# Transposed attention weights kept in their own tiles, and one stretch of value products per unit

## The chip, the cores and the metric

The kernel runs on one core of a Trainium2 chip. The metric is the device time of one execution in microseconds (us). Everything below is read from one profiled execution of the kernel before, and from its three timed runs.

## The reference, cut to what matters

A two-layer backbone over 1024 latent tokens and 256 context tokens, model width 1024, all in fp32. Each layer has two sub-layers. The first projects the tokens, runs three head groups beside each other (a gated mixer, a windowed attention, a differential attention) and projects their outputs back; the second is a gated MLP with a small convolution. Two of the head groups are attention, and only their last step is touched here:

```python
# B: windowed attention, 8 query heads over 2 kv heads, head width 64
p = softmax(concatenate([s_win, s_ctx, s_sink], axis=-1))
o = einsum('bnhgqk,bnkhd->bnqhgd', p_win, vb) + einsum('bnhgqk,bkhd->bnqhgd', p_ctx, v_ctx)
# C: differential attention, 4 heads, value width 64, all 1280 keys (context tokens read 256)
pd = p[:, :, 0] - lam * p[:, :, 1]
o  = einsum('bhqk,bkhd->bqhd', pd, v)
```

## The kernel before, in words

The kernel is written as a data-flow program; a scheduler orders the instructions of every engine when the kernel is built, by its own estimate of when each becomes ready, with the program's order as priority. So attention, which stands early in the program, is laced with matmuls of the projections and the MLP wherever attention isn't ready. On the chip each engine then follows its own fixed list.

Attention works in units over pairs of 128-token query tiles (`nq` is 2 everywhere). In `units_b` a unit is one kv head of one pair (18 units), and each unit has two blocks (`hp`), each with two query heads; a query tile sees 2 to 5 key tiles of 128. In `units_c` a unit is one head of one pair (36 units); a query tile sees 10 key tiles, or 2 for the context pair.

The path of a unit is the same in both. TensorE writes scores into PSUM tiles `S`; VectorE copies them negated into score tiles in SBUF with a running minimum (`negmax`, L496); ScalarE turns them into exponentials in place (L587, L703); in C, VectorE combines the two maps into the first one (L709). The score tiles are `pb` (B, one per query tile and block) and `ec` (C, two per query tile, `es[0]` and `es[1]`); both come from the same ring of four buffers, tag "e". They hold queries on partitions and keys in columns, and the value product needs keys on partitions. So `outputs` transposes them with TensorE, 128x128 at a time, into one of two PSUM tiles `T` (L609 in B, L734 in C); ScalarE copies a `T` tile into an SBUF tile `PT` (L613, L736), of which there are three; and TensorE multiplies the values with it into the PSUM tile `O` (L619, L725), accumulating over the key tiles. A product holds 64 value columns as weights, and the two query tiles of a pair go to partitions 0 to 63 and 64 to 127 of `O`. Transposes and products alternate: while ScalarE copies step k, TensorE is meant to do the products of step k-1. At the end of a B unit, four more matmuls with 64 weight columns (L629, `bc`) spread the reciprocal sums, and the result goes through `ob` and `stb`, which share the three buffers of tag "PT".

A `T` step in B is one key tile of both query tiles and both heads; in C it is four key tiles of one query tile. Matmuls of the projections and the MLP write PSUM tiles `z` and `zS` (L130, L132).

Of the kernel before, what the change touches and what calls it, by code (L numbers as in the profile page):

```python
# [10 lines left out]
F32 = mybir.dt.float32  # L11
F32R = mybir.dt.float32r
BF16 = mybir.dt.bfloat16
AF = mybir.ActivationFunctionType
# [18 lines left out]
P = 128  # L33
# [19 lines left out]
def trunk(ctx: ExitStack, tc: tile.TileContext, a: dict):  # L53
    nc = tc.nc
    act, dve, pool, pe, sp = nc.scalar, nc.vector, nc.gpsimd, nc.tensor, nc.sync

    def mkpool(name, bufs, side="left", space=None):
        kw = {"space": space} if space is not None else {}
        return tc.alloc_tile_pool(name=name, bufs=bufs, side=side, reuse_waits="tile", **kw)
# [10 lines left out]
    ident = cst[:, 0:P]  # L70
# [17 lines left out]
    st = {"wd": 0}  # L88
# [19 lines left out]
    def sub(eng, lo, src, hi):  # L108
        eng.tensor_tensor(out=lo, in0=src, in1=hi.bitcast(F32), op=ALU.subtract)  # L109
# [397 lines left out]
    def units_b(L, tiles, at, mkS, mkT, mkO):  # L507
# [3 lines left out]
        nq = len(tiles)  # L511
        cc = nwt * P
        info = []
# [5 lines left out]
        def unit(g):  # L519
# [24 lines left out]
            def scores():  # L544
# [3 lines left out]
                for hp in range(2):  # L548
                    pp = []
                    for ti, n in enumerate(tiles):  # L550
# [40 lines left out]
                        for j in (2 * hp, 2 * hp + 1):  # L591
                            pool.tensor_scalar(out=dgs[ti][:, j], in0=ident, scalar1=ls[:, j:j + 1], scalar2=None,  # L592
                                               op0=ALU.mult)
                    outputs(hp, pp)

            def outputs(hp, pp):
                V = both["V"]
                if hp == 0:
                    u["po"] = mkO()
                po = u["po"]  # L600
                prev = None
                for kk in range(max(len(x_[1]) for x_ in info) + 1):
                    tis = [ti for ti in range(nq) if kk < len(info[ti][1])]
                    new = None
                    if tis:
                        tp = mkT()
                        for m, ti in enumerate(tis):
                            for j in range(2):
                                pe.transpose(tp[:, (2 * m + j) * P:(2 * m + j) * P + P],  # L609
                                             pp[ti][:, j, kk * P:kk * P + P], ident)  # L610
                        PT = at.tile([P, 512], F32, tag="PT", name="PT", bufs=3)
                        w_ = 256 * len(tis)
                        act.activation(out=PT[:, :w_], in_=tp[:, :w_], func=AF.Copy)  # L613
                        new = (kk, tis, PT)
                    if prev is not None:
                        pk, ptis, pPT = prev
                        for m, ti in enumerate(ptis):
                            ix = info[ti][1]
                            pe.matmul(po[64 * ti:64 * ti + 64, 256 * hp:256 * hp + 256],  # L619
                                      V[:, ix[pk], 64 * g:64 * g + 64], pPT[:, 256 * m:256 * m + 256],  # L620
                                      start=(pk == 0), stop=(pk == len(ix) - 1))
                    prev = new
                if hp == 0:
                    return
                dgs = u["dg"]
                np_ = 64 * nq
                bc = mkT()
                for ti in range(nq):
                    pe.matmul(bc[64 * ti:64 * ti + 64, :], ones[:, 0:64], dgs[ti].rearrange("p j t -> p (j t)"),  # L629
                              start=True, stop=True)  # L630
                ob = at.tile([P, 512], F32, tag="PT", name="ob", bufs=3)
                act.activation(out=ob[:np_], in_=po[:np_], func=AF.Copy)
                dve.tensor_tensor(out=ob[:np_], in0=bc[:np_], in1=ob[:np_], op=ALU.mult)
                st = [at.tile([P, 512], F32R, tag="PT", name="stb", bufs=3) for _ in range(2)]
                act.activation(out=st[0][:np_], in_=ob[:np_], func=AF.Copy)
                sub(pool, st[1][:np_], ob[:np_], st[0][:np_])
                for ti, n in enumerate(tiles):
                    for h in range(2):
                        r0 = 256 + 256 * g
                        sp.dma_start(out=o_s[L][h, r0:r0 + 256, n * P:n * P + P].rearrange("(g d) t -> d g t", d=64),  # L640
                                     in_=st[h][64 * ti:64 * ti + 64].bitcast(F32).rearrange("d (g t) -> d g t", t=P))
# [6 lines left out]
    def units_c(L, hd, groups, at, mkS, mkT, mkO):  # L648
        kall = groups[0][0] < NLT
        k0 = 0 if kall else SEQ  # L650
        nk = NT - k0
        nkt = nk // P
        head = {}

        def unit(gi, tiles):
            nq = len(tiles)
# [22 lines left out]
            def scores():  # L679
# [3 lines left out]
                for ti in range(nq):  # L683
# [8 lines left out]
                    for bank in full[:h] + [rest] + full[h:]:  # L692
# [4 lines left out]
                        for b, (m, o, w_) in enumerate(bank):  # L697
# [4 lines left out]
                            if left[m] == h + 1:  # L702
# [7 lines left out]
                                                    in1=es[0][:, :nk], op0=ALU.mult, op1=ALU.add)  # L710
                    Ps.append(es[0])
                outputs(Ps)

            def outputs(Ps):
                V = head["V"]
                po = mkO()
                todo = [(q0, ti) for q0 in range(0, nkt, 4) for ti in range(nq)]
                PTs, ready = {}, []

                def pv():  # L720
                    q0 = ready.pop(0)
                    nb = min(4, nkt - q0)
                    for b in range(nb):
                        for ti in range(nq):
                            pe.matmul(po[64 * ti:64 * ti + 64, 0:P], V[:, q0 + b, :],  # L725
                                      PTs[q0, ti][:, b * P:b * P + P],
                                      start=(q0 + b == 0), stop=(q0 + b == nkt - 1))
                    return nb * 233.0

                for q0, ti in todo:  # L730
                    nb = min(4, nkt - q0)
                    tp = mkT()
                    for b in range(nb):
                        pe.transpose(tp[:, b * P:b * P + P], Ps[ti][:, (q0 + b) * P:(q0 + b) * P + P], ident)  # L734
                    PT = PTs[q0, ti] = at.tile([P, 512], F32, tag="PT", name="PT", bufs=3)
                    act.activation(out=PT[:, :nb * P], in_=tp[:, :nb * P], func=AF.Copy)  # L736
                    cost = nb * 107.0
                    if ready:
                        cost += pv()
                    if ti == nq - 1:  # L740
                        ready.append(q0)
                pv()
                nr = 64 * nq
                on = at.tile([P, P], F32, tag="on", name="on")
                act.activation(out=on[:nr], in_=po[:nr, 0:P], func=AF.Copy)
                tail(on)
# [168 lines left out]
    def finish(L, G, xg, mp):  # L915
# [5 lines left out]
        for (tok, xc, n) in G["out"]:  # L921
            for o in range(0, n, P):
# [24 lines left out]
               out=[(0, 0, 127), (SEQ, 128, 256)]),  # L947
# [4 lines left out]
               out=[(511, 0, 513)])]  # L952
# [14 lines left out]
    mkT = lambda: psT.tile([P, 512], F32, tag="T", name="T", bufs=2)  # L967
# [106 lines left out]
    at = mkpool("at0", 2, "left")  # L1074
# [105 lines left out]
    at = mkpool("at1", 2, "left")  # L1180
# [102 lines left out]
```

## Time and profile before

| | us |
|---|---|
| median of three timed runs | 3327.45 (3325.96 to 3328.93) |
| profiled execution, its own time | 3326.23 |
| span of the profiled execution | 3324.4 |
| TensorE matmul busy | 3146.2 (95%) |
| TensorE weight load busy | 2745.6 (83%) |
| VectorE busy | 2348.0 (71%) |
| ScalarE busy | 1744.8 (52%) |
| GpSimd busy | 888.1 (27%) |

The span is the time from the first to the last recorded instruction; the execution's own time has 1.83 us more. Matmuls are pipelined, so a matmul's duration in a row is longer than the step from one matmul to the next; where a cost on TensorE matters, it is read from starts, not from durations.

### The profile page before, as it was taken

How to read it: one execution, taken by the hardware profiler on the slowest of the kernel's cores; microseconds unless marked ns; L12 is line 12 of the kernel's file. 1: busy time of each engine (PE TensorE's matmuls, PEld its weight loads, DVE VectorE, ACT ScalarE, POOL GpSimd, SP SyncE). 2: the span in 40 equal slices, each digit the busy share in tenths (PEclk: the TensorE clock that was granted, in tenths of full speed). 3: DMA queues.
4: the chain of work that ended last, by engine and by line, in shares of the span. 5: the costliest groups of instructions: out<-in, count | busy, mean ns of one | idle time of the engine just before them, and what ended most of it. 6: DMA issues, size and time to landing. Idle time of an engine off the chain costs nothing. (4 is left out here: it accounts for less than half of the span.)

```text
span 3324.4 us, 54575 instructions
## 1 busy us (share of the span) xinstructions
PE 3146.2 (95%) x19503; PEld 2745.6 (83%) x19503; DVE 2348.0 (71%) x5306; ACT 1744.8 (52%) x3059; POOL 888.1 (27%) x1170
## 2 busy tenths in 40 slices
PE   7999989899999999999999899999999999999999
PEld 4776556787898889988999777767887789999999
DVE  5776666766878695878776678748776685666666
ACT  3554545655556563646444345557665564454443
POOL 1545211123222470127101054222322323222000
PEclk8999999899999999999999999999999999999999
DMA  8655786344533763378333556455645536434433
GB/s 270 187 162 156 225 250 180 86 128 122 136 106 89 241 177 114 105 199 238 102 96 113 169 144 171 125 150 151 163 138 152 135 110 195 122 106 137 137 114 109
DMA packets 754127, 499.52 MB, mean 150 GB/s; under 512 B 81480, under 2 KB 697792, under 8 KB 753856
## 3 DMA queue, kind: packets, MB, share of 16 engines
q1 hardware_dynamic: 753856, 496.03, 52.2%
q8 instruction: 155, 2.54, 0.3%
q14 instruction: 116, 0.95, 0.1%
HBM read 432.48 MB, written 63.44 MB: 149 GB/s over the span
## 5 line engine op out<-in xcount | busy, mean ns | idle before, releaser
L130 PE MATMUL z<-h,wsp 128*128 128x386 f32 (+3 forms) x5280 | 872.9, 319 | 17.2 <-ACT wsp L115 4.3
L130 PEld LDWEIGHTS z<-h,wsp 128*128 128x128 f32 x5280 | 823.8, 190 | 34.0 <-issue 11.4
L115 ACT ACTIVATE wsp<-raw 128x1024 fp32r<-128x1024 f32 (+2 forms) x660 | 556.0, 845 | 414.1 <-PE z L130 181.7
L109 DVE TENSOR_TENSOR wsp<-raw,wsp 128x1024 fp32r<-128x1024 f32 (+2 forms) x516 | 566.3, 1100 | 101.8 <-ACT wsp L115 98.5
L130 PE MATMUL z<-g,wsp 128*128 128x386 f32 (+3 forms) x2640 | 453.8, 320 | 18.0 <-DVE t L874 5.3
L130 PEld LDWEIGHTS z<-g,wsp 128*128 128x128 f32 x2640 | 412.9, 190 | 33.2 <-issue 10.0
L132 PE MATMUL z<-wsp,h 128*128 128x512 f32 x1584 | 401.1, 400 | 13.3 <-ACT zs L435 4.8
L109 POOL TENSOR_TENSOR wsp<-raw,wsp 128x128 fp32r<-128x128 f32 x528 | 253.7, 513 | 485.6 <-ACT wsp L115 439.4
L132 PEld LDWEIGHTS z<-wsp,h 128*128 128x128 f32 x1584 | 291.2, 190 | 80.3 <-ACT zs L435 7.0
L130 PE MATMUL zS<-h,wsp 128*128 128x386 f32 (+1 forms) x2112 | 334.2, 314 | 11.2 <-DVE t L874 4.3
L130 PEld LDWEIGHTS zS<-h,wsp 128*128 128x128 f32 x2112 | 319.0, 191 | 14.5 <-ACT wsp L115 5.1
L867 ACT ACTIVATE t<-z,cw 128x386 f32<-128x386 f32 (+3 forms) x220 | 137.8, 627 | 220.1 <-PE z L130 219.0
L871 DVE SCALAR_TENSOR_TENSOR t<-z,cw,t 128x255 f32<-128x255 f32 (+3 forms) x264 | 132.6, 502 | 150.9 <-ACT t L867 150.8
L496 DVE TENSOR_SCALAR_CACHE_REDUCE ec<-S,nmc 128x512 f32<-128x512 f32 (+1 forms) x256 | 173.9, 679 | 71.3 <-PE S L695 68.2
L171 POOL TENSOR_TENSOR mev<-mev,mtr 128x512 f32<-128x512 f32 x112 | 176.9, 1593 | 136.9 <-ACT mtr L170 134.1
L703 ACT ACTIVATE ec<-ec,nmc 128x1280 f32<-128x1280 f32 (+1 forms) x144 | 182.2, 1266 | 58.9 <-DVE ec L496 56.0
L130 PE MATMUL z<-oT,wsp 128*128 128x384 f32 (+2 forms) x1056 | 201.3, 337 | 2.5 <-DMA oT<-o_s 2.5
L899 DVE SCALAR_TENSOR_TENSOR xg<-z,mods,xg 128x384 f32<-128x384 f32 (+5 forms) x288 | 139.9, 501 | 81.3 <-PE z L130 79.9
L130 PE MATMUL zS<-g,wsp 128*128 128x386 f32 (+1 forms) x1056 | 181.8, 316 | 8.7 <-ACT g L884 4.0
L130 PEld LDWEIGHTS z<-oT,wsp 128*128 128x128 f32 x1056 | 178.8, 190 | 10.1 <-ACT zs L435 2.0
L381 POOL TENSOR_TENSOR rs<-ss,cst 128x8 f32<-128x8 f32 (+1 forms) x76 | 117.4, 1545 | 241.3 <-DVE ss L379 157.0
L592 POOL TENSOR_SCALAR dgb<-cst,ls 128x128 f32<-128x128 f32 x144 | 92.0, 652 | 317.9 <-DVE ls L590 168.1
(248 smaller groups left out, 4811.4 us busy)
## 6 DMA issues: line engine op xcount, KB each, us to landing
raw<-in_w_up_dram SPq DMA_DIRECT2D x264, 512.0 KB
mraw<-in_w_ada_dram SPq DMA_DIRECT2D x96, 512.0 KB
raw<-in_w_down_dram SPq DMA_DIRECT2D x192, 256.0 KB
Kc<-qk_s SPq DMA_DIRECT2D x96, 320.0 KB
raw<-in_w_in_dram SPq DMA_DIRECT2D x52, 512.0 KB
raw<-in_w_out_dram SPq DMA_DIRECT2D x48, 512.0 KB
raw<-in_w_down_dram SPq DMA_DIRECT2D x104, 192.0 KB
qk_s<-st SPq DMA_DIRECT2D x18, 512.0 KB
```

The costliest lines, as they stand in the source:

```text
L109: eng.tensor_tensor(out=lo, in0=src, in1=hi.bitcast(F32), op=ALU.subtract)
L115: act.activation(out=hl[:, 0], in_=raw, func=AF.Copy)
L130: pe.matmul(ps, w(i, k), h(j, k), start=s, stop=e)
L132: pe.matmul(ps, h(i, k), w(j, k), start=s, stop=e)
L171: pool.tensor_tensor(out=acc[s], in0=acc[s], in1=pr, op=ALU.add)
L381: pool.tensor_tensor(out=rs[:, :ns], in0=ss[:, 1, :ns], in1=mhalf[:, :ns], op=ALU.pow)
L496: dve.tensor_scalar(out=neg, in0=s_ap, scalar1=-1.0, scalar2=init, op0=ALU.mult, op1=ALU.min, accum_out=acc)
L592: pool.tensor_scalar(out=dgs[ti][:, j], in0=ident, scalar1=ls[:, j:j + 1], scalar2=None, op0=ALU.mult)
L703: act.activation(out=es[m][:, :nk], in_=es[m][:, :nk], func=AF.Exp, scale=-1.0, bias=acc[m], accum_out=l1[:, m, ti:ti + 1])
L867: act.activation(out=t[:, o:o + n], in_=ps[:, :n], func=AF.Identity, scale=cw[:, L, 1, ft:ft + 1], bias=cw[:, L, 3, ft:ft + 1])
L871: dve.scalar_tensor_tensor(out=t[:, o + b + 1:o + e], in0=ps[:, b:e - 1], scalar=cw[:, L, 0, ft:ft + 1], in1=t[:, o + b + 1:o + e], op0=AL ...
L899: dve.scalar_tensor_tensor(out=xs, in0=ps[:, b + o0:b + o1], scalar=mods[:, L, 40 + ct, s:s + 1], in1=xs, op0=ALU.mult, op1=ALU.add)
```

## The change

In both functions the copies that ScalarE makes of the transposed weights no longer go to a `PT` tile: they overwrite the score tile's own columns that were just transposed. All transposes and copies of a unit (in B: of a block) stand first, and after them all its products with the values, beginning with the last key tile and the last query tile, and with the pair's two query tiles side by side. In B a `T` tile now holds two key tiles of one query tile instead of one key tile of both. `ob` and `stb` get buffers of their own (one each, `stb` twice as wide), which take the 6 KB a partition that the three `PT` buffers had.

```diff
@@ units_b, outputs @@
-                prev = None
-                for kk in range(max(len(x_[1]) for x_ in info) + 1):
-                    tis = [ti for ti in range(nq) if kk < len(info[ti][1])]
-                    new = None
-                    if tis:
+                for k0 in range(0, max(len(x_[1]) for x_ in info), 2):
+                    for ti in range(nq):
+                        nb = min(2, len(info[ti][1]) - k0)
+                        if nb <= 0:
+                            continue
                         tp = mkT()
-                        for m, ti in enumerate(tis):
-                            for j in range(2):
-                                pe.transpose(tp[:, (2 * m + j) * P:(2 * m + j) * P + P],
-                                             pp[ti][:, j, kk * P:kk * P + P], ident)
-                        PT = at.tile([P, 512], F32, tag="PT", name="PT", bufs=3)
-                        w_ = 256 * len(tis)
-                        act.activation(out=PT[:, :w_], in_=tp[:, :w_], func=AF.Copy)
-                        new = (kk, tis, PT)
-                    if prev is not None:
-                        pk, ptis, pPT = prev
-                        for m, ti in enumerate(ptis):
-                            ix = info[ti][1]
+                        for j in range(2):
+                            for b in range(nb):
+                                pe.transpose(tp[:, (j * nb + b) * P:(j * nb + b + 1) * P],
+                                             pp[ti][:, j, (k0 + b) * P:(k0 + b + 1) * P], ident)
+                        act.activation(out=pp[ti][:, :, k0 * P:(k0 + nb) * P],
+                                       in_=tp[:, :2 * nb * P].rearrange("p (j c) -> p j c", j=2), func=AF.Copy)
+                for b in range(max(len(x_[1]) for x_ in info)):
+                    for ti in reversed(range(nq)):
+                        ix = info[ti][1]
+                        kk = len(ix) - 1 - b
+                        if kk >= 0:
                             pe.matmul(po[64 * ti:64 * ti + 64, 256 * hp:256 * hp + 256],
-                                      V[:, ix[pk], 64 * g:64 * g + 64], pPT[:, 256 * m:256 * m + 256],
-                                      start=(pk == 0), stop=(pk == len(ix) - 1))
-                    prev = new
+                                      V[:, ix[kk], 64 * g:64 * g + 64], pp[ti][:, :, kk * P:kk * P + P],
+                                      start=(b == 0), stop=(kk == 0))
...
-                ob = at.tile([P, 512], F32, tag="PT", name="ob", bufs=3)
+                ob = at.tile([P, 512], F32, tag="ob", name="ob", bufs=1)
...
-                st = [at.tile([P, 512], F32R, tag="PT", name="stb", bufs=3) for _ in range(2)]
+                st = at.tile([P, 2, 512], F32R, tag="stb", name="stb", bufs=1)
+                st = [st[:, 0], st[:, 1]]
@@ units_c, outputs @@
-                todo = [(q0, ti) for q0 in range(0, nkt, 4) for ti in range(nq)]
-                PTs, ready = {}, []
-                def pv():
...
-                for q0, ti in todo:
-                    nb = min(4, nkt - q0)
-                    tp = mkT()
-                    for b in range(nb):
-                        pe.transpose(tp[:, b * P:b * P + P], Ps[ti][:, (q0 + b) * P:(q0 + b) * P + P], ident)
-                    PT = PTs[q0, ti] = at.tile([P, 512], F32, tag="PT", name="PT", bufs=3)
-                    act.activation(out=PT[:, :nb * P], in_=tp[:, :nb * P], func=AF.Copy)
-                    cost = nb * 107.0
-                    if ready:
-                        cost += pv()
-                    if ti == nq - 1:
-                        ready.append(q0)
-                pv()
+                for q0 in range(0, nkt, 4):
+                    for ti in range(nq):
+                        nb = min(4, nkt - q0)
+                        tp = mkT()
+                        for b in range(nb):
+                            pe.transpose(tp[:, b * P:b * P + P], Ps[ti][:, (q0 + b) * P:(q0 + b) * P + P], ident)
+                        act.activation(out=Ps[ti][:, q0 * P:(q0 + nb) * P], in_=tp[:, :nb * P], func=AF.Copy)
+                for kt in reversed(range(nkt)):
+                    for ti in reversed(range(nq)):
+                        pe.matmul(po[64 * ti:64 * ti + 64, 0:P], V[:, kt, :], Ps[ti][:, kt * P:kt * P + P],
+                                  start=(kt == nkt - 1), stop=(kt == 0))
```

## Rows read from the trace of the kernel before

**Rows 1.** The page, part 1: busy time, share of the span, instructions.

```profile
PE 3146.2 (95%) x19503; PEld 2745.6 (83%) x19503; DVE 2348.0 (71%) x5306; ACT 1744.8 (52%) x3059; POOL 888.1 (27%) x1170
```

**Rows 2.** Windows of attention stages: PE, PEld, DVE, ACT, POOL busy; PEclk; DMA.

```profile
560.00:680.00 120.00, 102.38 (x598) 83.40 (x596) 91.91 (x250) 75.00 (x141) 22.10 (x28) 0.86 0.41 110
680.00:840.00 160.00, 159.43 (x990) 129.41 (x989) 101.98 (x299) 89.02 (x162) 44.46 (x84) 1.00 0.49 129
840.00:960.00 120.00, 118.90 (x737) 107.83 (x736) 94.22 (x231) 66.31 (x109) 19.40 (x35) 1.00 0.45 123
...
2140.00:2300.00 160.00, 149.10 (x1036) 105.72 (x1037) 97.61 (x341) 102.55 (x202) 42.93 (x57) 0.97 0.58 162
2300.00:2440.00 140.00, 130.44 (x1050) 117.09 (x1049) 118.25 (x287) 89.80 (x162) 38.27 (x75) 1.00 0.57 153
```

**Rows 3.** Tile O: the products, durations in ns (least/median/most), first and last start.

```profile
L725 PE MATMUL O<-PT,Vc x1312: 272/273/477, 195.6 to 2750.5; 128*64 128x128 f32 x188
...
L619 PE MATMUL O<-PT,Vb x640: 379/430/690, 288.4 to 2622.1; 128*64 128x256 f32 x160
```

**Rows 4.** Timeline of PE in a B block: start us, us, what, count.

```profile
341.56 0.66 PE L609 MATMUL T<-cst,pb 128*128 128x128 f32 x4
342.14 0.65 PE L619 MATMUL O<-PT,Vb 128*64 128x256 f32 x4
342.72 0.44 PE L609 MATMUL T<-cst,pb 128*128 128x128 f32 x2
```

**Rows 5.** Timeline of PE around a longer B stretch.

```profile
310.61 1.08 PE L619 MATMUL O<-PT,Vb 128*64 128x256 f32 x8
311.62 1.09 PE L609 MATMUL T<-cst,pb 128*128 128x128 f32 x8
```

**Rows 6.** Timeline of PE in a C unit.

```profile
881.01 1.09 PE L725 MATMUL O<-PT,Vc 128*64 128x128 f32 x14
882.03 0.87 PE L734 MATMUL T<-cst,ec 128*128 128x128 f32 x6
882.83 0.43 PE L725 MATMUL O<-PT,Vc 128*64 128x128 f32 x2
883.20 3.91 PE L130 MATMUL z<-h,wsp 128*128 128x384 f32 x21
...
892.64 0.65 PE L725 MATMUL O<-PT,Vc 128*64 128x128 f32 x6
893.22 1.48 PE L130 MATMUL z<-h,wsp 128*128 128x384 f32 x7
```

**Rows 7.** Timeline of PE: first and last of 192 C stretches.

```profile
195.56 0.43 PE L725 MATMUL O<-PT,Vc 128*64 128x128 f32 x2 [0.47 <-ACT PT L736]
...
2750.09 0.65 PE L725 MATMUL O<-PT,Vc 128*64 128x128 f32 x6
```

**Rows 8.** Timeline of PE: first and last of 171 B stretches.

```profile
288.36 0.65 PE L619 MATMUL O<-PT,Vb 128*64 128x256 f32 x4
...
2621.85 0.59 PE L619 MATMUL O<-PT,Vb 128*64 128x256 f32 x2
```

**Rows 9.** Groups by line and shape: the copies of T (busy us, mean ns; idle before).

```profile
L613 ACT ACTIVATE PT<-T 128x512 f32<-128x512 f32 x152 | 88.8, 592 | 95.7 <-PE T L609 82.4 <-DMA o_s<-stb 8.5 <-POOL stb L109 4.4
...
L736 ACT ACTIVATE PT<-T 128x512 f32<-128x512 f32 x128 | 73.9, 592 | 46.5 <-PE T L734 42.1 <-DMA o_s<-stb 1.8 <-DMA qc<-qk_s 1.8
...
L736 ACT ACTIVATE PT<-T 128x256 f32<-128x256 f32 x72 | 27.3, 380 | 46.2 <-PE T L734 46.1
```

**Rows 10.** Waits of VectorE: engine, line, for what: us in total, times, longest.

```profile
DVE pb L561 <- PE T L609: 42.6, 25, 9.0
...
DVE ec L496 <- PE T L734: 13.9, 13, 2.7
DVE pb L561 <- PE T L734: 13.8, 9, 4.3
```

More of the change, by code (lines that the diff above doesn't have):

```diff
@@ L716, in outputs @@
                 po = mkO()
-                todo = [(q0, ti) for q0 in range(0, nkt, 4) for ti in range(nq)]
-                PTs, ready = {}, []
-                def pv():
-                    q0 = ready.pop(0)
-                    nb = min(4, nkt - q0)
-                    for b in range(nb):
[L724 to L728, printed above, removed]
-                for q0, ti in todo:
-                    nb = min(4, nkt - q0)
-                    tp = mkT()
-                    for b in range(nb):
-                        pe.transpose(tp[:, b * P:b * P + P], Ps[ti][:, (q0 + b) * P:(q0 + b) * P + P], ident)
-                    PT = PTs[q0, ti] = at.tile([P, 512], F32, tag="PT", name="PT", bufs=3)
-                    act.activation(out=PT[:, :nb * P], in_=tp[:, :nb * P], func=AF.Copy)
-                    cost = nb * 107.0
-                    if ready:
-                        cost += pv()
-                    if ti == nq - 1:
-                        ready.append(q0)
-                pv()
+                for q0 in range(0, nkt, 4):
[9 more added lines that the diff above has]
+                                  start=(kt == nkt - 1), stop=(kt == 0))
                 nr = 64 * nq
```

## The prediction

> **What bounds the kernel now.** I read the page's busy times first. TensorE's matmuls cover 95% of the span, VectorE 71%, ScalarE 52% [rows 1]; the reader should note that this is an average over very different stages, and that a busy TensorE isn't yet a TensorE doing products. So next come the windows of the stages with attention [rows 2]. In 680 to 840 and 840 to 960 TensorE is busy for 159.43 of 160 and 118.90 of 120 us, at a granted clock of 1.00 (the 2.4 GHz level): whatever attention leaves free is filled with matmuls of the projections and the MLP. In 2140 to 2300 and 2300 to 2440 it idles for 10.9 of 160 and 9.6 of 140 us. In 560 to 680 it idles for 17.6 of 120 us, at a clock of 0.86. In the same windows VectorE is at 61 to 84% and ScalarE at 55 to 64%. So mostly TensorE is the limit, the others close enough behind that its idle time would grow if its work shrank.
>
> The third view is the order on TensorE, where one sees what the busy time is made of. Four transposes between two stretches of products take 0.58 us from start to start, six take 0.80 [rows 4, 6]: 0.11 each, and 0.14 once. Four B products take 0.58, eight take 1.01 [rows 4, 5]: two products for the two query tiles run together in 0.215, and 0.15 comes on top once. C products take 0.37, 0.58 and 1.02 for two, six and fourteen [rows 6]: 0.11 per two, and 0.26 once. The fixed parts belong to the change between matmuls with 128 and with 64 weight columns: each excursion to the products and back costs about 0.15 + 0.14 = 0.29 us in B and 0.26 + 0.14 = 0.40 in C, in which no result is made. That the fixed part of C is 0.11 larger, just one pair, suggests (an estimate) that in each C stretch two products of one query tile follow each other and don't run together.
>
> How often does that happen? Going through the whole timeline I counted 192 stretches of C products [rows 7] and 171 of B products [rows 8]. There are 1312 and 640 products [rows 3], so a stretch has 6.8 or 3.7 products on average, while a full C unit has 20 and a full B block up to 10.
>
> **The change, part by part.** *Alternation removed.* Now the excursions cost 192 x 0.40 = 77 us and 171 x 0.29 = 50 us, 127 us of TensorE time. After it the first product needs the copy that comes last (in C always, in B but for the eight blocks of pair (6, 7), whose first product may start alone), so when it can run all others of the unit can, and they have priority over the later work that fills gaps. I expect 36 C stretches and 36 B stretches (the L629 matmuls also have 64 columns and follow the second block's products): 36 x 0.40 + 36 x 0.29 = 25 us. That frees 102 us of TensorE time. If the scheduler cut every stretch in two, another 25 us would be lost; if the pairs all run together, 4 us more are gained.
>
> *Copies.* In C their number and size stay. In B there are 184 for 168: 136 of 512 columns and 48 of 256, for 152 and 16. At 592 and 380 ns [rows 9] (the 256-column price from C) that is 98.7 us for 96.1: +2.6 us on ScalarE, hidden behind its idle 36 to 45% [rows 2]. They write two pieces per row in B, which no row shows: at best nothing, at worst two copies of 256, 0.76 for 0.592, 23 us in all on ScalarE, also under that cover. I take nothing, since the element count is the same.
>
> *Products read from the score tile.* In B the moving operand is two pieces of 128 columns. Two C pairs of 128 take 0.22, one B pair of 256 takes 0.215 [rows 5, 6], so even as two halves it costs nothing. I take nothing.
>
> *Own buffers for `ob` and `stb`.* Copies no longer wait for a store or GpSimd to free a `PT` buffer: 8.5 + 4.4 + 1.8 us of ScalarE's idle time [rows 9]. ScalarE isn't the limit; I take nothing, and at most 15 us.
>
> *New waits.* TensorE no longer has products to do while ScalarE empties `T`, and the product stretch waits for a last copy. Behind that wait all of TensorE's list is queued. The score tiles are also held longer: until the last product, not the last transpose. That is one copy and one stretch later, 0.59 + 10 x 0.11 + 0.26 = 1.95 us in C and 0.59 + 5 x 0.215 + 0.15 = 1.8 us in B. Whoever wants the ring's next buffer waits: VectorE already does so for 42.6 + 13.9 + 13.8 us in 47 waits [rows 10], with its MLP work queued behind.
>
> *From TensorE time to the span.* Two bounds: all 102 us, if something always fills, and nothing, if the waits take it back. In stages like 680 to 960, with 1.7 us idle in 280, I expect about 0.8 of the freed time to shorten the stage: VectorE's 94.22 us still fit under the 112 us that 120 would become after 20 stretches at 0.40 are gone. In stages that idle 7 to 15% already (2140 to 2440, 560 to 680) I expect about 0.4. Both kinds hold a similar number of stretches, so 0.6: 61 us. Against the profiled execution's own 3326.23 us that gives 3265 us. The median of the timed runs, 3327.45, is 1.2 us higher, so the sum stands for either.
>
> **The rivals.**
>
> *All of it arrives: 3224 us.* For it: 118.90 of 120 us busy at full clock, and the filled work would have to be done later anyway. Against it: VectorE at 84% in 2300 to 2440, whose share would pass 90%.
>
> *The copies set the pace: 3325 us.* A full unit has four copies of 512 and two of 256, 4 x 0.592 + 2 x 0.380 = 3.13 us, and only 20 x 0.11 = 2.2 us of transposes; with two `T` tiles TensorE must wait for the 0.93 us between. Before, products stood there. Uncovered in the 64 units and blocks that read latent tokens that is 60 us, and eats the 61. For it: copies and transposes wait on each other already. Against it: the order is made when the kernel is built, and has other matmuls to put there, as it does between the C stretches at 883.20 and 893.22 [rows 6]. The Trainium skill has the rule for this: "TensorEngine Tiling (Array Packing)", section "PSUM Bottleneck", says that column tiling speeds up TensorE and not the emptying of PSUM, so that the copy out of PSUM may become the bottleneck, and advises sharing it between ScalarE and VectorE, which this change doesn't do. By that rule the time would be 3325; the rows agree only in that 3.13 is more than 2.2.
>
> *The held score tiles decide: about 3354 us, slower.* If each of the 47 waits for the ring grows by 1.9 us and VectorE's lateness reaches TensorE each time, that costs 89 us against the 61. For it: 70 us of such waits exist [rows 10]. Against it: a C unit's ti = 0 can take the two `es[1]` buffers, which are still freed by L709. It decides from some 32 waits of 1.9 us on that no other matmul covers.
>
> *The products don't stay in one stretch.* With two pieces each, 77 us are freed and 0.6 of that is 46: 3280, inside the forecast's range.
>
> **How the numbers follow.** The forecast (with 3280) gets 0.64, all of it 0.14, the copies 0.10, the held tiles 0.12. A run of this kernel can tell from no change what is over about 0.2%, 6.7 us. The copies' case is split: 0.07 same, 0.02 faster, 0.01 slower. So faster 0.80, same 0.07, slower 0.13. The range goes from 3218 (all of it, the 4 us of pairs and a little of the 15 us of buffers) to 3325 (the copies); it leaves out the held tiles and the half of the copies' case that lies above. The forecast's own range is 3230 to 3300.
>
> **What would show it.** Right: about 72 stretches of products (L619 and L725 by their new lines) in place of 363, each 1.1 to 1.4 us long; the sum of "issue" idle before transposes and products much smaller; TensorE's matmul busy time some 100 us lower; the attention stages over sooner. The filling share is seen in TensorE's idle in the windows: it should rise by some 40 us in all. Wrong: VectorE's waits for the score ring, now put down to products, at 150 us or more; transposes that wait for copies by tens of us; or far more than 72 stretches. The prediction fails if the fixed 0.14 and 0.15 belong to something other than the change of the column count, or if the new order that the scheduler makes loses elsewhere more than it gains here.

## The result: 43 us faster, inside the forecast's range, 20 us short of its number

The changed kernel takes 3284.61 us in the median of four runs (3280.13 to 3288.13), the kernel before 3327.86 beside it. The ratio is 0.987, with a 95% interval of 0.9853 to 0.9887. The profiled execution has a span of 3280.3 us. Forecast were 3265 us, with a range of 3218 to 3325.

The page's first part, as in [rows 1]:

```profile
PE 3072.3 (94%) x19503; PEld 2754.6 (84%) x19503; DVE 2330.4 (71%) x5306; ACT 1742.7 (53%) x3075; POOL 892.2 (27%) x1170
```

TensorE's busy time fell by 73.9 us, and its idle time in the span rose from 178.2 to 208.0, by 29.8: 73.9 - 29.8 = 44.1 us, which is the difference of the two spans. So part of what was freed came back as idle.

The order on TensorE, in the timeline of a C unit (first fence) and of a B block (second), to be set against [rows 4 to 6]:

```profile
881.58 0.60 PE L724 MATMUL T<-cst,ec 128*128 128x128 f32 x4
...
883.72 4.43 PE L130 MATMUL z<-h,wsp 128*128 128x384 f32 x24
888.09 2.40 PE L729 MATMUL O<-ec,Vc 128*64 128x128 f32 x40
890.42 0.73 PE L696 MATMUL S<-Kc,qc 128*128 128x256 f32 x3
```

```profile
331.02 0.66 PE L610 MATMUL T<-cst,pb 128*128 128x128 f32 x4 [0.27 <-ACT pb L612]
331.81 2.37 PE L620 MATMUL O<-pb,Vb 128*64 128x256 f32 x18
334.12 0.66 PE L610 MATMUL T<-cst,pb 128*128 128x128 f32 x4
```

A C unit's products now stand in one stretch, of 40 records in the 32 latent units and of 8 in the four context units; before, the longest had 16. The copies that the products wait for are covered by 24 matmuls of `z`. Counted through the timeline there are 36 stretches of C products and 48 of B, 84 in place of 363. A stretch of 40 lasts 888.09 to 890.42, 2.3 us, and not the 1.1 to 1.4 that were forecast. The reason is in the program: a latent C unit issues 20 products and leaves 40 records, so each of these fp32 products is two records. The 1312 and 640 records of [rows 3] are 656 and 320 products. The steps of 0.11 and 0.215 were thus those of a pair of records (two starts 7 ns apart, the next pair 0.109 us later in C) and not of a pair of whole products. The 0.11 by which C's fixed part is larger is, as the estimate had it, a product of one query tile without a partner: the last two of the 14 records at 881.01 in [rows 6] start 0.109 us apart. The cost of an excursion and the number of excursions, on which the sum rests, don't depend on how many records a product leaves.

What ended the idle time of weight loads before transposes and products, in the list of waits (us in total, times, longest), after in the first fence and before in the second:

```profile
PEld T L610 <- issue: 13.7, 32, 0.8
...
PEld O L620 <- issue: 6.7, 29, 0.4
...
PEld T L724 <- issue: 6.0, 7, 4.1
...
PEld O L729 <- issue: 4.0, 15, 0.4
```

```profile
PEld T L609 <- issue: 55.6, 141, 0.8
...
PEld O L725 <- issue: 27.5, 127, 0.8
...
PEld O L619 <- issue: 21.3, 87, 1.6
PEld T L734 <- issue: 14.4, 73, 1.3
```

These four sum to 30.4 us after and 118.8 before. This is the same removal seen by another view: 88.4 us of pauses for which no awaited engine is shown.

The third view is no view of the profile but an account of my own, made from the starts of all 19503 matmuls. For each step from one start to the next I took what it exceeds the median step between two matmuls of that form in a row (for value products, whose records run in pairs, half the step of a pair), and put it into a class:

| excess over the usual step, us | before | after | |
|---|---|---|---|
| into 64-column matmuls, out of them, and the first step behind | 121.8 | 32.2 | -89.6 |
| products without a partner, inside the stretches | 17.2 | 4.2 | -13.0 |
| single steps over 0.45 us too long (waits) | 204.7 | 231.8 | +27.1 |
| small delays between two `z` matmuls | 54.0 | 66.7 | +12.7 |
| all other steps, the scores' among them | -12.4 | 4.6 | +17.0 |
| sum | 385.3 | 339.6 | -45.7 |

The first two lines are what the change removes: 102.6 us, where 102 were forecast. Of these 56.8 came back in the three lines below. Part of that is the granted clock: TensorE stood at the 1.2 GHz level for 137 us of the execution before and for 173 of the one after, and about half of the growth of the last two lines lies in steps made at that level.

**Where the rest went.** Windows of after, with the columns of [rows 2]:

```profile
560.00:680.00 120.00, 99.72 (x583) 87.89 (x584) 90.88 (x243) 73.56 (x137) 28.69 (x42) 0.83 0.41 112
680.00:840.00 160.00, 160.00 (x1056) 140.03 (x1055) 104.95 (x313) 94.01 (x177) 44.41 (x80) 1.00 0.49 132
840.00:960.00 120.00, 117.32 (x759) 112.52 (x758) 95.65 (x242) 67.67 (x112) 24.18 (x47) 0.99 0.48 130
...
2140.00:2300.00 160.00, 151.10 (x1204) 126.38 (x1203) 110.96 (x347) 110.08 (x219) 50.85 (x75) 0.99 0.54 149
2300.00:2440.00 140.00, 127.52 (x1082) 120.00 (x1081) 117.34 (x282) 91.73 (x163) 39.18 (x77) 0.99 0.65 166
```

Read the counts, not the busy times: between 680 and 840 TensorE is full before and after, and now starts 1056 matmuls there instead of 990; between 2140 and 2300 it is 1204 for 1036. Between 560 and 680 it is 583 for 598: nothing is won, and the granted clock is 0.83 for 0.86, more of the window at the 1.2 GHz level. To see where the time is won for good I compared the start of the k-th `z` or `zS` matmul in both traces. The gain is +22 us at k = 1800 (741 us before), +36 at 3000 (1075 us), +18 at 3600 (1199 us), about +25 through the MLP of the first layer, +43 at 9000 (2221 us), +57 at 10200 (2496 us) and +45 from 2800 us to the end. So some 18 us are given back where the first layer's attention ends (7 of them return by k = 3900), and 12 at the end of the second's. In the first of these places, after:

```profile
1100.00:1120.00 20.00, 17.35 (x99) 17.00 (x97) 19.03 (x25) 13.86 (x24) 15.73 (x10) 0.99 0.44 137
1120.00:1140.00 20.00, 16.89 (x77) 16.05 (x77) 19.35 (x27) 14.43 (x25) 16.94 (x11) 0.84 0.76 248
1140.00:1160.00 20.00, 12.52 (x54) 11.55 (x55) 10.16 (x11) 11.99 (x18) 14.34 (x11) 0.84 1.08 356
```

VectorE is busy for 38.4 of the first 40 us, then the DMA engines are full (a share of 1.08), and TensorE has 46.8 of 60. What limits there isn't TensorE any more. The 300 `z` and `zS` matmuls from k = 3300 to 3600 show it. Before they took 55.4 us, with TensorE idle for 1.2 and 0.7 at the 1.2 GHz level. After they took 74.7, with 13.2 idle and 17.1 at 1.2 GHz. Of the 13.2 us, 10.2 are waits for `wsp`, the weight tiles that ScalarE and VectorE have to split first (L115, L109). So 12 of the 19 us given back here are idle time, 9 of them added waiting for these weights, and the other 7 stand beside the lower clock. Why the weights are late there isn't shown.

The wait that grew most is the one of C's scores for a PSUM tile that VectorE has not yet copied out, in the list of waits of TensorE (matmul, then weight load), after and before:

```profile
PE S L696 <- DVE ec L496: 27.2, 31, 4.0
...
PEld S L696 <- DVE ec L496: 41.2, 45, 4.5
```

```profile
PE S L695 <- DVE ec L496: 12.6, 21, 2.1
...
PEld S L695 <- DVE ec L496: 24.7, 34, 2.3
```

The matmuls' part is +14.6 us, half of the 29.8 us by which TensorE idles more.

### The profile page after: what moved, and what is told of

Same layout as the page of the kernel before. It is cut to its first block, busy times and chain, and to the rows that moved or that the text cites. A ratio compares the mean times of both kernels' runs of the same rounds, so it can differ in the third digit from the quotient of the medians.

```text
span 3280.3 us, 54515 instructions
## 1 busy us (share of the span) xinstructions
PE 3072.3 (94%) x19503; PEld 2754.6 (84%) x19503; DVE 2330.4 (71%) x5306; ACT 1742.7 (53%) x3075; POOL 892.2 (27%) x1170
## 4 chain that ended last, share of the span: by engine, by line
PE 64%; DVE 11%; DMA 8%; ACT 4%; POOL 3%; issue 3%; SPq 1%; ACTq 0%; POOLq 0%; DVEq 0%
PE z L130 32%; PE zS L130 11%; PE z L132 6%; PE O L620 2%; DVE wsp L109 2%; DMA raw<-in_w_up_dram 2%; DMA mraw<-in_w_ada_dram 2%; PE T L610 2%; PE O L729 2%; DVE ec L496 2%; PE S L696 1%; POOL mev L171 1%; POOL wsp L109 1%; PE zS L132 1%; PE T L724 1%
## 5 line engine op out<-in xcount | busy, mean ns | idle before, releaser
L115 ACT ACTIVATE wsp<-raw 128x1024 fp32r<-128x1024 f32 (+2 forms) x660 | 555.7, 845 | 423.7 <-PE z L130 185.2
L109 DVE TENSOR_TENSOR wsp<-raw,wsp 128x1024 fp32r<-128x1024 f32 (+2 forms) x516 | 562.6, 1092 | 108.2 <-ACT wsp L115 105.2
L109 POOL TENSOR_TENSOR wsp<-raw,wsp 128x128 fp32r<-128x128 f32 x528 | 258.5, 522 | 426.6 <-ACT wsp L115 358.4
L696 PE MATMUL S<-Kc,qc 128*128 128x512 f32 (+1 forms) x400 | 143.6, 401 | 35.0 <-DVE ec L496 27.2
```

The lines of the kernel that those rows point to most:

```text
L115: act.activation(out=hl[:, 0], in_=raw, func=AF.Copy)
L696: pe.matmul(S[:, b * w_:b * w_ + w_], q[:, m, ti * P:ti * P + P], K[m][:, o:o + w_], start=True, stop=True)
```

## The experiments

Ratios are to the kernel before, run on the same chip beside the experiments; its median was 3326.23 us beside e1 to e4, 3327.62 beside e5 to e8 and 3326.89 beside e9 to e12. In e1 to e4 "theory 1" is that of the prediction; in the others each expectation states its own.

**e1 and e2: each half alone.** e1 has the change in `units_c` only, e2 in `units_b` only (its loops, with `ob` and `stb` still on the three buffers of tag "PT" that C uses).

```diff
@@ e1: units_c as in the change, units_b as before @@
-                    PT = PTs[q0, ti] = at.tile([P, 512], F32, tag="PT", name="PT", bufs=3)
-                    act.activation(out=PT[:, :nb * P], in_=tp[:, :nb * P], func=AF.Copy)
...
+                        act.activation(out=Ps[ti][:, q0 * P:(q0 + nb) * P], in_=tp[:, :nb * P], func=AF.Copy)
...
@@ e2: units_b's loops as in the change, units_c as before @@
-                for kk in range(max(len(x_[1]) for x_ in info) + 1):
...
+                for k0 in range(0, max(len(x_[1]) for x_ in info), 2):
...
+                for b in range(max(len(x_[1]) for x_ in info)):
+                    for ti in reversed(range(nq)):
...
```

> Only the differential attention (C) is changed; the windowed attention (B) stays as before. Stretches of C products fall from 192 to 36, those of B stay. Theory 1 (the change between 128 and 64 weight columns is what is saved, and about 0.43 of the freed TensorE time reaches the span, as in the changed kernel): 156 x 0.40 = 62 us freed, about 27 us faster, 3301. Theory 2 (the gain comes from B and from the own buffers of ob and stb): within 8 us of the kernel before.

> Only the windowed attention (B) is changed, and ob and stb keep sharing the three PT buffers with C; C stays as before. Stretches of B products fall from 167 to 44. Theory 1: 123 x 0.29 = 36 us freed, about 15 us faster, 3313, and the two parts add up to the whole 43. Theory 2 (B and the own buffers make the gain): over 25 us faster, or, if it is the buffers, no gain at all here.

e1 took 3328.99 us, ratio 1.0009 (1.0001 to 1.0018): nothing is won. e2 took 3313.77, ratio 0.9962 (0.9948 to 0.9975), 12 us faster, as theory 1 had it. In the account of steps e1 did remove what it should: switching 121.8 to 72.7 and products without a partner 17.2 to 1.0, 65 us. But its waits went from 204.7 to 244.4 and the small delays between `z` matmuls from 54.0 to 73.5, which takes 59 of the 65 back. The clock has a share in that: TensorE stood at the 1.2 GHz level for 223 us of e1's profiled execution, against 137 before, and nearly all that the small `z` delays grew lies in steps at that level. The list of waits of e1:

```profile
PEld T L609 <- issue: 59.2, 143, 1.2
PEld S L695 <- DVE ec L496: 46.8, 52, 4.5
```

B's pauses stand as before, and the scores' wait for VectorE is at 46.8 for 24.7. So in this order of the program, TensorE time that is freed in C alone isn't worth anything to the span. A constant share, the prediction's 0.6 or the 0.43 that theory 1 uses, is wrong: the share depends on what else is late. (In a second order, e7 below, C alone does gain.)

**e3: one stretch, but from the first key.** The products stand behind the transposes as in the change, but run from the first key tile and the first query tile up.

```diff
-                    for ti in reversed(range(nq)):
+                    for ti in range(nq):
                         ix = info[ti][1]
-                        kk = len(ix) - 1 - b
-                        if kk >= 0:
+                        kk = b
+                        if kk < len(ix):
...
-                for kt in reversed(range(nkt)):
-                    for ti in reversed(range(nq)):
+                for kt in range(nkt):
+                    for ti in range(nq):
...
```

> The changed kernel, but its products begin with the first key tile and the first query tile. In the order made when the kernel is built there are then 306 excursions to products with 64 columns, against 355 before and 91 in the changed kernel; tiles, copies and buffers are those of the changed kernel. Theory 1 (the excursions are what counts): 49 fewer than before at 0.3 to 0.4 are 15 to 20 us freed, 6 to 9 us faster than before, 3319 to 3322. Theory 2 (no PT tiles, own buffers, bigger T steps make the gain): within 10 us of the changed kernel, 3285.

It took 3347.34 us, ratio 1.0062 (1.0049 to 1.0076), 21 us slower than the kernel before and 63 slower than the changed one; neither theory had that. A product from the first key needs only the first copy, so the scheduler starts it early and fills in between: the program's order on TensorE has 306 excursions to 64-column matmuls, the changed kernel's 91, the one before's 355. Switching is at 104.3 us, but products without a partner are at 28.8 (before 17.2) and waits at 213.1. The pauses are back:

```profile
PEld O L729 <- issue: 26.4, 134, 0.8
```

So the order of the keys isn't a detail: it is what makes the scheduler keep a stretch whole. By these three classes e3 is within 3 us of the kernel before; the rest of its loss, some 20 us, is spread over ordinary steps. Most of that lies in steps at the 1.2 GHz level, at which e3 spends 166 us for 137; what brings it there I haven't found. (e3 also turns the order of the two query tiles round; e12 below does that alone and keeps the gain.)

**e4: the same program with 128 weight columns in C.** It is the kernel before, with each C product loading two key tiles' values side by side and writing 128 partitions. It leaves out the accumulation over the key tiles, so C doesn't put out the attention output, and only the times are read.

```diff
-                            pe.matmul(po[64 * ti:64 * ti + 64, 0:P], V[:, q0 + b, :],
+                            v0 = max(q0 + b - 1, 0)
+                            pe.matmul(po[:, P * ti:P * ti + P], V[:, v0:v0 + 2, :].rearrange("p k d -> p (k d)"),
                                       PTs[q0, ti][:, b * P:b * P + P],
-                                      start=(q0 + b == 0), stop=(q0 + b == nkt - 1))
+                                      start=True, stop=True)
```

> The kernel before, but each C product takes 128 weight columns (the values of two key tiles) and writes 128 partitions, each as an accumulation of its own; so what C puts out is not the attention output, and only the times are read. B is untouched and stands beside it as it was. Theory 1 (the fixed cost belongs to the change of the column count): from four transposes to C products 0.44 us in place of 0.58, and n matmuls of C products take n x 0.11 with nothing on top; B keeps its 0.15 and 0.14. The time rises all the same, since two query tiles no longer run side by side: 656 x 0.11 = 72 us more, less 192 x 0.29 = 56. Theory 2 (the fixed cost belongs to the change of the operands or of the PSUM bank): C keeps 0.14 and 0.15 around each stretch.

It took 3358.12 us in a single run, 32 above the kernel before, where theory 1 added up 16. The total says little, since every product has twice the weights and pairs no longer run side by side; the timeline says what was asked:

```profile
904.39 0.60 PE L735 MATMUL T<-cst,ec 128*128 128x128 f32 x4
904.83 0.39 PE L726 MATMUL O<-PT,Vc 128*128 128x128 f32 x2
904.97 1.11 PE L130 MATMUL z<-h,wsp 128*128 128x384 f32 x5
...
908.66 1.72 PE L726 MATMUL O<-PT,Vc 128*128 128x128 f32 x14
910.22 0.60 PE L735 MATMUL T<-cst,ec 128*128 128x128 f32 x4
```

Four transposes ahead of products take 0.44 us from start to start (0.58 in [rows 4]), two product records 0.14, fourteen 1.56, which is 14 x 0.111. Both fixed parts are gone, while C's products still alternate with transposes as before. In the list of waits, B, which keeps 64 columns, keeps its pauses:

```profile
PEld T L609 <- issue: 56.4, 140, 0.8
```

Nor is it the accumulation that e4 leaves out: in the same trace the L629 matmuls don't accumulate either and keep 64 weight columns, and from their last pair to a matmul with 128 it is 0.53 us, against 0.43 between two of their pairs. That shows that the cost belongs to the change of the column count. "TensorEngine Tiling (Array Packing)", section "Key Properties", of the Trainium skill says that a change of tiling mode drains TensorE; this case agrees in that each change costs about 0.15 us.

**e5 to e8: the same four kernels in another order.** Is 43 us the change, or an accident of one order? The table that gives the additions of the norm stage to VectorE or ScalarE was turned round, which moves 12 instructions from ScalarE to VectorE and shifts the whole order; attention isn't touched. e5 is the kernel before with it, e6 the changed one, e7 and e8 the halves.

```diff
-AD = "mmmmd"
+AD = "dmmmm"
```

> The kernel before with one setting outside attention changed (the first layer's first norm tiles scale on VectorE and not partly on ScalarE, the last norm tiles of the second layer the other way). That moves some 0.5 us operations between two engines, and the scheduler makes another order from there on; excursions to products are 361 for 355. Theory 1 (the time of a kernel like this is set by its TensorE work and its waits, and an order that differs by accident matters little): within 8 us of the kernel before. Theory 2 (C's missing gain in the run with C alone comes from the accident of that order): 10 to 25 us off either way.

> The changed kernel with the same setting; 91 excursions as in the changed kernel. Theory 1: about 43 us faster than the kernel before with that setting. Theory 2: the gain over it lies anywhere between 15 and 70 us.

> The change in C alone with the same setting; 201 excursions. Theory 1 (C's freed TensorE time is always taken back by waits, since C isn't bound by TensorE): within 8 us of the kernel before with that setting. Theory 2 (the zero was an accident of one order): 15 to 35 us faster than it.

> The change in B alone with the same setting; 242 excursions. Theory 1: 10 to 18 us faster than the kernel before with that setting, as without it. Theory 2: anywhere between 5 slower and 35 faster.

| us, median | first order | second order |
|---|---|---|
| before | 3327.86 | 3337.57 (1.0034: 1.0020 to 1.0049) |
| C alone | 3328.99 | 3323.03 (0.9986: 0.9976 to 0.9996) |
| B alone | 3313.77 | 3323.95 (0.9992: 0.9982 to 1.0001) |
| both | 3284.61 | 3289.36 (0.9889: 0.9874 to 0.9903) |

Against the kernel before of its own order the whole change gains 43 and 48 us, C alone -1 and 15, B alone 14 and 14 (against 3327.86 and 3337.57; against the 3326.23 beside which they ran, C alone is at -3 and B alone at 12). The whole gain stands in both orders, as theory 1 of e6 and e8 had it. The kernel before itself moves by 10 us, more than theory 1 of e5 allowed, and C alone gains 15 us in the second order and not nothing, so theory 1 of e7 is wrong: the zero of e1 belongs to one order. The single halves vary by up to 16 us with an edit that has nothing to do with them, and in the change both together gain 30 (43 - 13) or 20 (48 - 28) us more than the sum of their single gains. Part of that may be that the halves leave `ob` and `stb` on the ring of `PT`. In e1 ScalarE does wait for that ring, for 6.4 us until a store of `stb` is done and for 4.4 until GpSimd has made a `stb`; in e2 no copy is seen to wait for either, so for B's half the ring explains nothing that is seen. A changed kernel with `ob` and `stb` on a shared ring, which would separate the buffers from the rest, wasn't run, and where the joint 20 to 30 us come from stays open.

**e9: every second copy on VectorE.** In the changed kernel the copies of the second query tile's transposes go to VectorE.

```diff
@@ units_b; in units_c likewise @@
...
+                        if ti:
+                            dve.tensor_copy(dst, src)
+                        else:
+                            act.activation(out=dst, in_=src, func=AF.Copy)
...
```

> The changed kernel, with the copies of the second query tile of each pair made by VectorE and not by ScalarE, so that the two engines share the emptying of T. Theory 1 (in C the late engine is VectorE, and TensorE's freed time ends in waits for it to empty the score banks): slower than the changed kernel by 5 to 40 us, since some 100 us of copies are added to it, and TensorE's waits for VectorE at the scores grow beyond 27 + 41 us. Theory 2 (the copies set the pace of the transposes): 10 to 30 us faster than the changed kernel.

3276.93 us (3272.04 to 3279.54), ratio 0.9845 (0.9828 to 0.9862): the fastest kernel of the study, about 8 us below the changed one, whose interval it overlaps by 0.0009; so the gain is likely, in this one order, but not clear of noise, and theory 2's 10 to 30 us aren't reached. That VectorE would become late by it, as theory 1 of this run had it, is wrong: its busy time rose from 2330.4 to 2413.1 us, while its waits for score tiles that products still hold fell from 73 to 47 us, and TensorE's waits for VectorE at the scores, which were to grow beyond 27 and 41 us, are 18.9 and 38.6. From e9's list of waits, the first line a new wait, and then three of the four groups of that old one (the fourth is 5.3 us):

```profile
DVE pb L615 <- PE T L610: 24.8, 25, 3.5
...
DVE pb L561 <- PE O L624: 23.4, 24, 2.5
...
DVE ec L496 <- PE O L737: 12.1, 11, 2.9
...
DVE pb L561 <- PE O L737: 6.3, 3, 2.5
```

The longest of the old ones are 2.5 to 3.9 us, and were up to 10.5. VectorE now also waits for transposes, for 24.8 us in B and 13.8 in C, and the kernel isn't slower for it. By which of these the 8 us come, no further run separates.

**e10 and e11: a third score bank.** To test whether the scores' wait for a PSUM tile is what eats the gain, e11 gives `S` a third bank. It takes it from `U`, which then shares the two `T` banks; e10 is the control with that sharing alone.

```diff
 e10 and e11
-    mkU = lambda: psT.tile([P, 512], F32, tag="U", name="U")
+    mkU = lambda: psT.tile([P, 512], F32, tag="T", name="U", bufs=2)
 e11 alone
-    psS = mkpool("psS", 2, "right", PSUM)
+    psS = mkpool("psS", 3, "right", PSUM)
```

> Control for the next run: the changed kernel, with the single PSUM tile U of the projections and norms put into the two-tile ring of T, so that one PSUM bank is left unused. Both theories: slower than the changed kernel by 0 to 20 us, since transposes of attention and of the projections then wait for each other.

> As the control, with the free bank given to the score tiles S (three in place of two). Theory 1 (the new waits are TensorE's at the scores, for VectorE to empty a bank): those waits fall from 27 + 41 us to under 30 in all, and the time is 10 to 30 us below the control's. Theory 2 (VectorE itself is the limit there, and a further bank only moves the wait): within 8 us of the control.

e10 took 3529.46 us, ratio 1.0617 (1.0588 to 1.0646), and e11 3531.37, 1.0610 (1.0593 to 1.0627). The control itself costs 245 us instead of 0 to 20. TensorE's idle time rose from 208 to 350 us and its busy time from 3072.3 to 3177.0, with 430 us at the 1.2 GHz level for 173. Among its waits the one for the scores grew most (first fence e10, second e11; 41.2 in the changed kernel):

```profile
PEld S L696 <- DVE ec L496: 99.6, 113, 3.6
...
PEld U L211 <- DVE red L209: 17.9, 4, 9.3
```

```profile
PEld S L696 <- DVE ec L496: 92.2, 107, 4.4
```

Against so disturbed a control the third bank gave nothing, and barely shortened the wait that it was meant for. That is theory 2's outcome, within 8 us of the control, and favours VectorE being late over the number of banks, but in a kernel 245 us away from the one in question; the pair is inconclusive for the changed kernel.

**e12: the first query tile first.** The changed kernel with the two query tiles of a pair in the other order, which lets some stretches start before the last copy.

```diff
-                    for ti in reversed(range(nq)):
+                    for ti in range(nq):
...
-                    for ti in reversed(range(nq)):
+                    for ti in range(nq):
```

> The changed kernel, products still from the last key tile, but with the first query tile ahead of the second. The first product then needs the copy before last, and in the order made when the kernel is built some products start alone: 137 excursions against 91. Theory 1 (excursions count, at about 0.3 us of TensorE time, of which some 0.43 reaches the span): 46 x 0.3 x 0.43 = 6 us slower than the changed kernel. Theory 2 (only the single stretch keeps the gain): as slow as with the first key tile first, 40 us or more above the changed kernel.

3281.43 us, ratio 0.9865 (0.9844 to 0.9886): the same as the changed kernel, though it has 137 excursions for 91. In the account of steps switching is at 48.3 us (32.2) and products without a partner at 20.0 (4.2), 32 us more on TensorE; waits are at 207.9 (231.8) and the small `z` delays at 58.2 (66.7), 32 us less. By the profile's page TensorE's busy time is 3096.9 us (3072.3) and its idle time 180.5 (208.0). Both theories had expected a loss; the 6 us of theory 1 are hardly more than the noise, the 40 of theory 2 are excluded. This is the clearest sign of where the gain stopped: in this run TensorE's own time and its waits trade one for one.

## Why the prediction was right, and where its number was off

- **The mechanism: right.** The fixed parts belong to the change between 64 and 128 weight columns (e4), and the freed TensorE time was 102.6 us by the account of steps, against 102. The count was 84 stretches for 72: the 12 more are the first products of the eight blocks of pair (6, 7), which the prediction named and didn't count. They start ahead of their stretch, and four of them as two records apart.
- **What a record is: wrong, without effect on the sum.** Two records are one product; a full stretch takes 2.3 us, not "1.1 to 1.4 us". It only made the time for which a score tile is held 1.1 us too short, and with it the price of the rival of the held tiles.
- **From TensorE time to the span: the step that was off.** 0.6 of the freed time was to shorten the span, 61 us; 43 to 44 of 102.6 did, 0.43. The step treats each stage by how full TensorE is; e1 and e12 show that it isn't a property of the stage: 65 us freed in C alone gave nothing in one order (and 15 in another), and 32 us put back on TensorE in e12 cost nothing that could be seen. TensorE's idle rose by 29.8 us where 40 were forecast, with a busy time 73.9 lower instead of "some 100". The remaining 29.7 us (12.7 + 17.0) are small delays in the account of steps. The prediction had no term for the granted clock, whose mean went from 0.980 to 0.974: 173 us of the execution at the 1.2 GHz level for 137, and about half of those 29.7 us are in steps at that level.
- **Nothing for the copies in two pieces: right.** The 512-column B copy takes 595 ns, for 592 in [rows 9]:

```profile
L612 ACT ACTIVATE pb<-T 128x512 f32<-128x512 f32 x136 | 78.3, 595 | 83.4 <-PE T L610 82.6
```

- **The held score tiles (3354): not borne out.** VectorE's waits for products that hold a tile, after:

```profile
DVE pb L561 <- PE O L620: 42.4, 27, 10.5
...
DVE ec L496 <- PE O L729: 16.1, 11, 4.6
...
DVE pb L561 <- PE O L729: 10.8, 3, 6.3
```

With a fourth of 3.7 us they make 73.0, against 70.3 in [rows 10] and not the 150 that would have decided. There are 45 of them for 47, so they aren't clearly longer either.
- **The copies set the pace (3325): a small part is true.** Weight loads of transposes and products that wait for copies are seen for 7.7 us and less a group, 20.6 in all, where 60 were needed and 21.0 stood before; `z` matmuls stand in the gap, as at 883.72. Sharing the copies won about 8 us, not clear of noise (e9), the direction of the advice in "TensorEngine Tiling (Array Packing)", section "PSUM Bottleneck", of the Trainium skill; but VectorE's waits for held tiles fell by 26 us in it, so the gain need not be TensorE waiting less for copies.
- **All of it arrives (3224): against it** stood VectorE's share, and VectorE is what TensorE waits for now in the group that grew most. Whether VectorE's lateness is the cause or only the next in line wasn't settled: e11 could not tell, and e9 gave VectorE 83 us more work and wasn't slower, so its total isn't what binds.

Open remain the joint 20 to 30 us of the halves, why the weights come late at the end of the first layer's attention, and a part of e3's loss.

## What to carry to other kernels

When matmuls with fewer weight columns alternate with full ones, read the cost of the change from starts of stretches of different length: the part that doesn't grow with the count is paid once per excursion, and ordering the work so that the excursion happens once is worth it. Make the dependency, not the priority, hold a stretch together: a first product that needs the last copy can't be started early by a scheduler. Don't credit freed time of a nearly full engine with a fixed share: here it was worth 0.43 for the whole change and, in one order, nothing for half of it, because idle time and steps at the lower clock took its place; and measure a gain of 10 us in a second order of the program before believing it.

## What the runs showed of the hardware

Each fp32 product of values and weights left two records (1312 for 656 in C), while an fp32 transpose left one. With 64 weight columns a pair of records of the two query tiles side by side takes 0.11 us (128 columns moving); with 128 weight columns it is 0.11 us for one record (e4). The change of the column count costs about 0.15 us each way. Of its execution TensorE stood at the 1.2 GHz level for 137 us in the kernel before, 173 in the changed one, 223 in e1 and 430 in e10. Letting the `U` tiles share the two `T` banks, which looked harmless, cost 245 us (e10).
